# A two-layer encoder trunk in float32 on one core: SwiGLU's gate and up products by Strassen's seven products, and w_down applied in four parts over its rows

## The chip, the cores and the metric

One Trainium2 chip, and one of its cores. A core has TensorE (PE in the rows; its weight loads are the rows PEld), VectorE (DVE), ScalarE (ACT), GpSimd (POOL), and SyncE (SP), which here only issues transfers. SBUF is the working memory of the engines, PSUM the memory into which TensorE accumulates. The metric is the device time of one execution in microseconds.

## What is computed

Two layers on 512 tokens of width 1024, batch 1. Layer 0 mixes tokens with an mLSTM, layer 1 with dilated window attention. Behind each mixer comes the part that the change touches:

```python
def swiglu(xn, w_gate, w_up, w_down):
    return (jax.nn.silu(xn @ w_gate) * (xn @ w_up)) @ w_down
...
        h = h + mix
        h = h + swiglu(rms_norm(h, norm_ffn[i]), w_gate[i], w_up[i], w_down[i])
        gate = jax.nn.sigmoid(rms_norm(h, norm_ple[i]) @ ple_gate[i])
        h = h + gate * (p[i] @ ple_proj[i])
```

`w_gate` and `w_up` are 1024 x 2816, `w_down` is 2816 x 1024, all in float32, a pair for each layer.

## The kernel before

The residual lives transposed in eight tiles `hT` of 128 channels x 512 tokens. Every product is done in three passes (`mm3`): each float32 operand is split into a rounded part (`hi`, `wh`) and a remainder (`lo`, `wl`), and TensorE adds hi·hi, hi·lo and lo·hi. The weights are split on the way: SyncE loads a stretch of up to 1024 rows x 256 columns into one of three buffers `wst` (line 107), ScalarE writes `wh` (line 116), VectorE writes `wl = wst - wh` (line 117), and TensorE multiplies. `wh` and `wl` have three buffers each. A splitting can therefore run at most two products ahead of TensorE, and a load can start only when a `wst` buffer has been read for the last time.

`colproj` (line 510) is a projection over 256-column stretches of a weight; `Norm.add` (line 174) splits the new residual, scaled by the norm's weight, as soon as one of its tiles is done, and adds its squares up. The factor of the norm itself (one for each token) is applied behind the product: `stats` makes the sums by TensorE, `rsqrt_cols` (lines 236 to 240) finishes them on GpSimd, and `bcast` sends them through DRAM (tile `rbd`) and back as `rB`, one row repeated on all partitions.

`ffn` (line 539) goes over 11 pairs of 128-column blocks of gate and up (below: a cell, 256 columns of each). Each block is 8 k-steps x 3 passes = 24 matmuls of 512 columns; the gate block is scaled (L550) and put through Silu (L551), the up block scaled (L557), multiplied (L558) and split (L560, L561). All 22 resulting tiles stay in SBUF, and then `w_down` is one `colproj` over all of them (22 k-steps in one accumulation), whose result is added to `hT`. A scheduler puts the instructions of each engine in a fixed order; each engine then works its own list strictly in that order, and waits on semaphores.

Of the kernel before, what the change touches and what calls it, by code (L numbers as in the profile page):

```python
# [11 lines left out]
F32 = mybir.dt.float32  # L12
# [14 lines left out]
KT = D // P  # L27
# [5 lines left out]
WST = 3  # L33


@with_exitstack
def encoder_kernel(
# [40 lines left out]
    def ut(shape=(P, S), dt=F32, tag="u", bufs=62):  # L78
        return up.tile(list(shape), dt, tag=tag, name=nm(tag), bufs=bufs)
# [7 lines left out]
    def f(t):  # L87
        return t.bitcast(F32)
# [73 lines left out]
    class Norm:  # L162


        def __init__(self, wcol, btiles=False):
            self.wcol = wcol
            self.xh, self.xl = [], []

            self.btiles = btiles
            self.bh, self.bl = [], []  # L170
            self.q = None
            self.rcol = None

        def add(self, k, square=True):
# [7 lines left out]
            if self.btiles:  # L182
# [348 lines left out]
    nf = Norm(NW_FFN)  # L531
# [3 lines left out]
    nf.stats()  # L535
    nf.bcast()


    def ffn(l, n, nxt, rows=True):
        ah, al = [], []  # L540
        for j2 in range(JT // 2):
            sg = wload(w_gate[l], 0, KT, 256 * j2)
            su = wload(w_up[l], 0, KT, 256 * j2)
            for cc in range(2):
                og_ = ps()
                wh, wl = wcols(sg, KT, cc)
# [369 lines left out]
    nf = Norm(NW_FFN + 8)  # L916
# [3 lines left out]
    nf.stats()  # L920
    nf.bcast()
# [127 lines left out]
```

## Time and profile before

| | us |
|---|---|
| median of 3 runs | 1663.88 (1663.49 to 1666.16) |
| the profiled execution | 1660.66 |
| its span, from the first to the last instruction | 1659.0 |
| TensorE busy | 1616.1 (97%) |
| VectorE, ScalarE, GpSimd busy | 812.6, 602.6, 373.7 |

The span is what the rows below are counted in; the profiled execution's own time has 1.66 us more. Busy is the sum of the instructions' times; matmuls overlap in it, so that the distance between the starts of two matmuls, and not their duration, says how fast TensorE goes.

### The profile page before, as it was taken

Reading aid. Unit: us, or ns where it says so; the run is one execution under the profiler, and the core shown is the slowest. Engines: PE = TensorE matmul, PEld = TensorE weight load, DVE = VectorE, ACT = ScalarE, POOL = GpSimd, SP = SyncE. Lnnn points to the kernel's source line nnn. Section 1 sums busy time; section 2 is a strip of 40 time slices with the busy share of each in tenths; the row PEclk is TensorE's granted clock in tenths of the full one; section 3 lists DMA queues with packets and bytes.
Section 4 is the critical chain, followed back from the end, with each engine's and each line's share of the span. In section 5 each row is a group of like instructions: output and inputs, shape, how many; then the busy total and the mean of one; then the engine's idle time right before and its main releaser. Section 6 shows DMA issues by size and latency. Waiting matters only on the chain.

```text
span 1659.0 us, 20883 instructions
## 1 busy us (share of the span) xinstructions
PE 1616.1 (97%) x8324; PEld 1378.0 (83%) x8324; DVE 812.6 (49%) x1369; ACT 602.6 (36%) x1026; POOL 373.7 (23%) x479
## 2 busy tenths in 40 slices
PE   6999999999999998999999999999999999999997
PEld 5898998788888887777898988988887888888886
DVE  7655654644443322834645645545434444433253
ACT  5666543423232322623242422424333332323242
POOL 4455402000000100205707537165020000001100
PEclk9999999999999999999999999999999999999999
DMA  5322222422223223313323223223223232232231
GB/s 169 115 77 77 77 79 76 132 82 98 89 90 127 96 76 64 114 58 111 93 52 103 76 65 114 53 82 97 78 76 124 87 100 83 97 126 96 83 103 51
DMA packets 182753, 151.13 MB, mean 91 GB/s; under 512 B 17448, under 2 KB 173152, under 8 KB 182656
## 3 DMA queue, kind: packets, MB, share of 16 engines
q1 hardware_dynamic: 181520, 149.61, 29.5%
q8 instruction: 65, 1.06, 0.3%
q14 instruction: 32, 0.26, 0.1%
q10 hardware_dynamic: 1104, 0.13, 0.1%
q0 software_dynamic: 32, 0.07, 0.0%
HBM read 147.60 MB, written 2.19 MB: 90 GB/s over the span
## 4 chain that ended last, share of the span: by engine, by line
PE 86%; DVE 5%; DMA 5%; ACT 2%; POOL 1%; issue 1%; POOLq 0%; SPq 0%; DVEq 0%; ACTq 0%
PE pj L125 21%; PE pj L126 21%; PE pj L124 21%; PE o L124 5%; PE o L125 5%; PE o L126 5%; PE o L458 2%; PE o L890 2%; DMA rbd<-rs 1%; DVE wl L117 1%; DMA u<-rbd 1%; PE s L879 1%; DMA swo<-swd 1%; DMA u<-in_positions_dram 1%; PE s L124 0%
## 5 line engine op out<-in xcount | busy, mean ns | idle before, releaser
L126 PE MATMUL pj<-u,wl 128*128 128x512 f32 x1336 | 521.6, 390 | 5.3 <-DVE wl L117 5.3
L125 PE MATMUL pj<-u,wh 128*128 128x512 f32 x1336 | 521.8, 391 | 2.5 <-DVE u L179 2.5
L124 PE MATMUL pj<-u,wh 128*128 128x512 f32 x1336 | 522.0, 391 | 0.0
L116 ACT CAST wh<-wst 128x1024 fp32r<-128x1024 f32 (+2 forms) x267 | 271.1, 1018 | 665.2 <-PE pj L125 429.8
L117 DVE TENSOR_TENSOR wl<-wst,wh 128x1024 fp32r<-128x1024 f32 (+2 forms) x263 | 320.3, 1220 | 201.0 <-ACT wh L116 200.6
L126 PEld LDWEIGHTS pj<-u,wl 128*128 128x128 f32 x1336 | 251.1, 188 | 58.7 <-DVE wl L117 7.3
L125 PEld LDWEIGHTS pj<-u,wh 128*128 128x128 f32 x1336 | 251.1, 188 | 54.9 <-DVE u L179 3.3
L124 PEld LDWEIGHTS pj<-u,wh 128*128 128x128 f32 x1336 | 251.3, 188 | 51.5
L197 POOL TENSOR_TENSOR u<-u,u 128x512 f32<-128x512 f32 x30 | 51.6, 1721 | 862.1 <-ACT u L193 862.1
L124 PE MATMUL pj<-wh,u 128*128 128x256 f32 (+1 forms) x576 | 171.7, 299 | 5.3 <-DVE u L372 3.3
L125 PE MATMUL pj<-wl,u 128*128 128x256 f32 (+1 forms) x576 | 172.5, 299 | 2.7 <-DVE wl L117 2.7
L126 PE MATMUL pj<-wh,u 128*128 128x256 f32 (+1 forms) x576 | 172.2, 299 | 0.0
L124 PE MATMUL o<-u,wh 128*128 128x512 f32 x368 | 143.2, 389 | 0.0
L125 PE MATMUL o<-u,wh 128*128 128x512 f32 x368 | 143.2, 389 | 0.0
L126 PE MATMUL o<-u,wl 128*128 128x512 f32 x368 | 143.2, 389 | 0.0
L750 POOL TENSOR_TENSOR u<-u,RS 32x512 f32<-32x512 f32 x48 | 85.4, 1779 | 203.5 <-DVE u L749 202.9
L124 PEld LDWEIGHTS pj<-wh,u 128*128 128x128 f32 x576 | 111.7, 194 | 9.0 <-DVE u L372 3.5
L125 PEld LDWEIGHTS pj<-wl,u 128*128 128x128 f32 x576 | 111.9, 194 | 6.7 <-DVE wl L117 4.0
L126 PEld LDWEIGHTS pj<-wh,u 128*128 128x128 f32 x576 | 111.9, 194 | 2.5
L557 DVE TENSOR_TENSOR u<-o,u 128x512 f32<-128x512 f32 x44 | 30.4, 691 | 129.5 <-PE o L126 129.5
L124 PEld LDWEIGHTS o<-u,wh 128*128 128x128 f32 x368 | 69.1, 188 | 14.5
L125 PEld LDWEIGHTS o<-u,wh 128*128 128x128 f32 x368 | 69.2, 188 | 14.2
(278 smaller groups left out, 1718.8 us busy)
## 6 DMA issues: line engine op xcount, KB each, us to landing
wst<-in_b_w_in_dram SPq DMA_DIRECT2D x48, 512.0 KB, 3.8
wst<-in_w_gate_dram SPq DMA_DIRECT2D x22, 1024.0 KB, 5.2
wst<-in_w_up_dram SPq DMA_DIRECT2D x22, 1024.0 KB, 5.4
wst<-in_w_down_dram SPq DMA_DIRECT2D x16, 1024.0 KB, 5.1
wst<-in_b_w_in_dram SPq DMA_DIRECT2D x12, 1024.0 KB, 5.1
wst<-in_a_w_in_dram SPq DMA_DIRECT2D x8, 1024.0 KB, 5.3
wst<-in_ple_gate_dram SPq DMA_DIRECT2D x8, 1024.0 KB, 5.1
wst<-in_w_down_dram SPq DMA_DIRECT2D x8, 768.0 KB, 4.4
```

Source lines behind the costliest of these rows:

```text
L116: A.copy(hi, src)
L117: eng.tensor_tensor(lo, src, f(hi), op=ALU.subtract)
L124: T.matmul(o, ah, bh, start=start, stop=False)
L125: T.matmul(o, ah, bl, start=False, stop=False)
L126: T.matmul(o, al, bh, start=False, stop=stop_)
L197: (G if k < KT - 1 else V).tensor_tensor(self.q, self.q, s, op=ALU.add)
L458: T.matmul(o[:, d, :], pt[d][s][:, j * P:(j + 1) * P], vt[s][:, hh, :], start=s == ks[0], stop=s == ks[-1])
L557: V.tensor_tensor(u, ou, n.rB, op=ALU.mult)
L750: G.tensor_tensor(sh, sh, RS, op=ALU.mult)
L879: T.transpose(tp[:, i * P:(i + 1) * P], src[i // 2][:, i % 2, sel * P:(sel + 1) * P], ident)
L890: T.matmul(a_tile(o[e], i) if bi < 2 else b_tile(o[e], i), vv[i][:, e * P:(e + 1) * P], pt[:, i * P:(i + 1) * P], start=bi == 0 and i == 0 ...
```

## The change

**Gate and up.** For each cell and each k-row half, w11 and w12 are the upper and lower 512 rows of the 256 gate columns, w21 and w22 those of the up columns. The tokens are cut into two halves of 256. The eight products (two weights, two k halves, two token halves) become seven (Winograd's form): w11 and w12 with the first token half, w22 and four sums of weights with sums of quadrants of the input. A product is now 2 column blocks x 4 k-steps x 3 passes = 24 matmuls of 256 columns, and 7 of them make a cell. The four weight sums `s_[0]`, `s_[1]`, `s_[3]`, `s_[2]` (here S0, S1, S3, S2) are made by GpSimd, 128 x 1024 elements each, in three buffers `sw`; each is then split like a weight. The input's sums are made and split in `Norm.sums` while the projection ahead of the FFN runs. Partial results go back and forth between PSUM and VectorE.

**w_down** is applied after 3, 6, 9 and 11 cells, to the 6, 6, 6 and 4 tiles made so far; each part is scaled by `rB`, and added to `hT` (by GpSimd in the first three parts, by VectorE in the last). So the factor of the norm is no longer applied in the up block.

**rB** is made by TensorE and not through DRAM, inside the first cell.

The diff, without the tail of `Norm.__init__`, the two call sites of layer 1 (the same as those of layer 0) and blank lines:

```diff
-    def ut(shape=(P, S), dt=F32, tag="u", bufs=62):
+    def ut(shape=(P, S), dt=F32, tag="u", bufs=56):
...
+            if self.quads:
+                self.sums(k, h, w)
             if square:
                 self.square(k)
+        def sums(self, k, h, w):
+            e = ut()
+            A.activation(e, h, AF.Copy, scale=w)
+            self.e.append(e)
+            lo, hi = slice(0, 256), slice(256, S)
+            if k < 4:
+                d = ut((P, 256))
+                self.d = getattr(self, "d", []) + [d]
+                V.tensor_tensor(d, e[:, hi], e[:, lo], op=ALU.subtract)
+                if k % 2 == 0:
+                    self.pair1 = ut(dt=F32R), ut(dt=F32R)
+                th, tl = (t[:, 256 * (k % 2):256 * (k % 2) + 256] for t in self.pair1)
+                A.copy(th, d)
+                V.tensor_tensor(tl, d, f(th), op=ALU.subtract)
+                self.th[k][0], self.tl[k][0] = th, tl
+                return
+            j = k - 4
+            d2, d3, d4 = (ut((P, 256)) for _ in range(3))
+            V.tensor_tensor(d2, e[:, hi], self.d[j], op=ALU.subtract)
+            V.tensor_tensor(d3, e[:, hi], self.e[j][:, hi], op=ALU.subtract)
+            V.tensor_tensor(d4, e[:, lo], d2, op=ALU.subtract)
+            for i, d in ((1, d2), (2, d3), (3, d4)):
...
+                A.copy(th, d)
+                V.tensor_tensor(tl, d, f(th), op=ALU.subtract)
+                self.th[j][i], self.tl[j][i] = th, tl
...
-    nf = Norm(NW_FFN)
+    nf = Norm(NW_FFN, quads=True)
     colproj(a_w_out[0], mh, ml, KT, residual(nf), D)
-    nf.stats()
-    nf.bcast()
...
     def ffn(l, n, nxt, rows=True):
-        ah, al = [], []
-        for j2 in range(JT // 2):
-            sg = wload(w_gate[l], 0, KT, 256 * j2)
-            su = wload(w_up[l], 0, KT, 256 * j2)
...
-        pt = ple_in(l)
-        colproj(w_down[l], ah, al, JT, residual(nxt), D)
+        def product(o, w4, xs, start):
+            wh, wl = wsplit(w4, (P, 4, 256))
+            for cc in range(2):
+                for k in range(4):
+                    xh, xl = xs(k)
+                    c = slice(cc * P, cc * P + P)
+                    for i, (a, b) in enumerate(((wh, xh), (wh, xl), (wl, xh))):
+                        T.matmul(o[:, cc], a[:, k, c], b, start=start and cc + k + i == 0,
+                                 stop=k == 3 and i == 2, skip_group_check=True)
...
+        def parts(u, hf, a):
+            for cc in range(2):
+                ah, al = a[cc]
+                A.copy(ah[:, half[hf]], u[:, cc])
+                V.tensor_tensor(al[:, half[hf]], u[:, cc], f(ah[:, half[hf]]), op=ALU.subtract)
+        def first(j):
+            c = {}
+            sg = wload(w_gate[l], 0, KT, 256 * j)
+            su = wload(w_up[l], 0, KT, 256 * j)
+            c["w"] = w11, w12, w21, w22 = sg[:, 0:4], sg[:, 4:8], su[:, 0:4], su[:, 4:8]
+            s_ = [wp.tile([P, 4, 256], F32, tag="sw", name=nm("sw"), bufs=NSW) for _ in range(4)]
+            c["s"] = s_
+            G.tensor_tensor(s_[0], w21, w22, op=ALU.add)
+            G.tensor_tensor(s_[1], s_[0], w11, op=ALU.subtract)
+            G.tensor_tensor(s_[3], w12, s_[1], op=ALU.subtract)
+            G.tensor_tensor(s_[2], w11, w21, op=ALU.subtract)
+            c["r1"] = ps("s", (P, 2, 256), 3)
+            product(c["r1"], w11, lambda k: blk(k, 0), True)
+            c["s1"] = wide()
+            A.copy(c["s1"], c["r1"])
+            r5 = ps("o", (P, 2, 256), 2)
+            product(r5, s_[0], tsum(0), True)
+            c["s15"] = wide()
+            V.tensor_tensor(c["s15"], c["s1"], r5, op=ALU.add)
+            return c
+        def middle(c):
+            w11, w12, w21, w22 = c["w"]
+            s_ = c["s"]
+            c["a"] = [(ut(dt=F32R), ut(dt=F32R)) for _ in range(2)]
+            product(c["r1"], w12, lambda k: blk(4 + k, 0), False)
+            c["r6"] = ps("pj", (P, 2, 256), 3)
+            product(c["r6"], s_[1], tsum(1), True)
+            if n.rB is None:
+                n.bcast(by_pe=True)
+            c["g"] = g = [wide(), wide()]
+            V.tensor_tensor(g[0], c["r1"], cols(0), op=ALU.mult)
+            A.activation(g[0], g[0], AF.Silu)
+            v = wide()
+            V.tensor_tensor(v, c["s15"], c["r6"], op=ALU.add)
+            r3 = ps("s", (P, 2, 256), 3)
+            product(r3, s_[3], lambda k: blk(4 + k, 1), True)
+            V.tensor_tensor(v, v, r3, op=ALU.add)
+            V.tensor_tensor(g[1], v, cols(1), op=ALU.mult)
+            A.activation(g[1], g[1], AF.Silu)
+            product(c["r6"], s_[2], tsum(2), False)
+            u = wide()
+            V.tensor_tensor(u, c["s15"], c["r6"], op=ALU.add)
+            V.tensor_tensor(u, u, g[1], op=ALU.mult)
+            parts(u, 1, c["a"])
+        def last(c):
+            product(c["r6"], c["w"][3], tsum(3), False)
+            u = wide()
+            V.tensor_tensor(u, c["s1"], c["r6"], op=ALU.add)
+            V.tensor_tensor(u, u, c["g"][0], op=ALU.mult)
+            parts(u, 0, c["a"])
+            return c["a"]
+        def down(j0, a, final):
+            for c2 in range(D // 256):
+                st = wload(w_down[l], 256 * j0, len(a), 256 * c2)
+                for cc in range(2):
+                    o = ps()
+                    wh, wl = wcols(st, len(a), cc)
+                    for k in range(len(a)):
+                        mm3(o, wh[:, k], wl[:, k], *a[k], k == 0, k == len(a) - 1)
+                    t, h = ut(), hT[2 * c2 + cc]
+                    V.tensor_tensor(t, o, n.rB, op=ALU.mult)
+                    (V if final else G).tensor_tensor(h, t, h, op=ALU.add)
+                    if final:
+                        nxt.add(2 * c2 + cc)
+        chunks = ((0, 3), (3, 6), (6, 9), (9, JT // 2))
+        cell = first(0)
+        n.stats()
+        for j0, j1 in chunks:
+            a = []
+            for j in range(j0, j1):
+                middle(cell)
+                done_ = cell
+                if j + 1 < JT // 2:
+                    cell = first(j + 1)
+                a += last(done_)
+            if j1 == JT // 2:
+                pt = ple_in(l)
+            down(j0, a, j1 == JT // 2)
```

TensorE's order in a steady cell is: w12, S1, S3, S2, then w11 and S0 of the next cell, then w22. In the rows below a name ends in a number of its own, and behind a row stands the engine or the transfer queue (DMAHW) whose semaphore it waits for. Lines are those of the changed kernel where nothing else is said.

First VectorE, in the middle of layer 0's gate and up. Of the kernel before, one gate and one up block (L117 is a split):

```order
L117 TENSOR_TENSOR wl_3698<-wst_3624,wh_3697 128x1024 [waits Activation_49]
L561 TENSOR_TENSOR u_3621<-u_3617,u_3620 128x512 [waits Activation_49]
L550 TENSOR_TENSOR u_3657<-pj_3628,u_2970 128x512 [waits PE_49]
L117 TENSOR_TENSOR wl_3730<-wst_3626,wh_3729 128x1024 [waits Activation_49]
L557 TENSOR_TENSOR u_3689<-o_3660,u_2970 128x512 [waits PE_49]
L558 TENSOR_TENSOR u_3689<-u_3689,u_3657 128x512 [waits DVE_49,Activation_49]
```

And of the change, from the split of S2 to the split of the next cell's w12 (L118 is the split; 4559 and 4561 are the next cell's gate and up weights, 4563 its S0):

```order
L118 TENSOR_TENSOR wl_4525<-sw_4322,wh_4524 128x1024 [waits Activation_49]
L652 TENSOR_TENSOR u_4490<-u_4388,pj_4457 128x512 [waits PE_49]
L118 TENSOR_TENSOR wl_4573<-wst_4559,wh_4572 128x1024 [waits DMAHW5_49,Activation_49]
L656 TENSOR_TENSOR u_4490<-u_4490,s_4492 128x512 [waits DVE_49,PE_49]
L657 TENSOR_TENSOR u_4487<-u_4490,u_3296 128x512 [waits DVE_49]
L118 TENSOR_TENSOR wl_4604<-sw_4563,wh_4603 128x1024 [waits Activation_49]
L662 TENSOR_TENSOR u_4552<-u_4388,pj_4457 128x512 [waits PE_49]
L663 TENSOR_TENSOR u_4552<-u_4552,u_4487 128x512 [waits DVE_49,Activation_49]
L118 TENSOR_TENSOR wl_4634<-wst_4318,wh_4633 128x1024 [waits DMAHW4_49,Activation_49]
L613 TENSOR_TENSOR u_4426<-u_4552,u_4425 128x256 [waits Activation_49]
L613 TENSOR_TENSOR u_4428<-u_4552,u_4427 128x256 [waits Activation_49]
L118 TENSOR_TENSOR wl_4673<-wst_4559,wh_4672 128x1024 [waits PE_49,Activation_49]
```

Before, two splits come with four other operations (L550, L557, L558, L561), and a cell has two such sets; now seven splits and thirteen other operations make a cell, and the split of w22 (4634) stands behind two operations that need S2's product.

Second GpSimd, where layer 0's FFN begins. Before, the last square is followed at once by the norm's factor (L236 to L240):

```order
L197 TENSOR_TENSOR u_2688<-u_2688,u_2915 128x512 [waits Activation_49,Pool_49]
L236 TENSOR_TENSOR rs_533_2961<-ms_532_2959,nhalf 128x4 [waits DVE_49]
L237 TENSOR_TENSOR rt_534_2962<-rs_533_2961 128x4 [waits Pool_49]
```

In the change, the second cell's S0 and S1 (L623, L624) and the issue of the positions' load stand between the last square (L241) and the factor (L280 to L284), and S0 waits for a load:

```order
L626 TENSOR_TENSOR sw_3148<-wst_3142,wst_3144 128x1024 [waits DVE_49]
L241 TENSOR_TENSOR u_2696<-u_2696,u_2995 128x512 [waits Activation_49,Pool_49]
L761 DMA u_3071<-in_positions_dram 32x512 [waits PE_49]
L623 TENSOR_TENSOR sw_3375<-wst_3373 128x1024 [waits DMAHW2_49,DVE_49]
L624 TENSOR_TENSOR sw_3376<-sw_3375,wst_3371 128x1024 [waits DMAHW1_49,DVE_49,Pool_49]
L280 TENSOR_TENSOR rs_596_3223<-ms_595_3221,nhalf 128x4 [waits DVE_49]
```

In layer 1 only S0 of the second cell stands ahead of the factor.

Third ScalarE at the end of the second part of three cells, where w_down begins (4911 is the first w_down load, L612 splits the last cell's results):

```order
L117 CAST wh_4876<-wst_4561 128x1024 [waits DMAHW6_49,PE_49,Activation_49]
L612 CAST u_4668<-u_4795 128x256 [waits DVE_49]
L612 CAST u_4670<-u_4795 128x256
L630 COPY u_4843<-s_4814 128x512 [waits PE_49]
L117 CAST wh_4914<-wst_4911 128x768 [waits DMAHW1_49,Activation_49]
L117 CAST wh_4940<-wst_4911 128x768 [waits PE_49,Activation_49]
L612 CAST u_4668<-u_4904 128x256 [waits DVE_49]
```

Since the next cell's gate and up already hold two of the three `wst` buffers, all four w_down loads of a part use one and the same buffer, which is the one whose last reader is the split of w22 (`wh_4876` and its `wl`). Before, the first w_down loads came while three buffers took turns.

## Rows read from the trace of the kernel before

**Rows 1.** The page: busy time and share by engine, then the chain that ended last.

```profile
PE 1616.1 (97%) x8324; PEld 1378.0 (83%) x8324; DVE 812.6 (49%) x1369; ACT 602.6 (36%) x1026; POOL 373.7 (23%) x479
...
PE 86%; DVE 5%; DMA 5%; ACT 2%; POOL 1%; issue 1%; POOLq 0%; SPq 0%; DVEq 0%; ACTq 0%
```

**Rows 2.** Stages: stretch, its length, busy time of each engine, clock, DMA.

```profile
300.00:475.00 175.00, 175.00 (x774) 144.91 (x773) 84.39 (x102) 54.04 (x68) 0.00 (x0) 1.00 0.30 97
```

**Rows 3.** Timeline of PE: start, duration; 512-column matmuls in `ffn`, 56 steps apart.

```profile
559.77 0.39 PE L126 MATMUL pj<-u,wl 128*128 128x512 f32 x1
...
572.47 0.39 PE L125 MATMUL pj<-u,wh 128*128 128x512 f32 x1
```

**Rows 4.** Timeline of PE in layer 0's gate projection: 256-column matmuls, 13 steps apart.

```profile
199.75 0.28 PE L125 MATMUL pj<-wl,u 128*128 128x256 f32 x1
...
201.31 0.28 PE L126 MATMUL pj<-wh,u 128*128 128x256 f32 x1
```

**Rows 5.** Timeline of DVE in `ffn`: back-to-back operations.

```profile
342.47 0.69 DVE L558 TENSOR_TENSOR u<-u,u 128x512 f32<-128x512 f32 x1
343.08 1.22 DVE L117 TENSOR_TENSOR wl<-wst,wh 128x1024 fp32r<-128x1024 f32 x1
344.22 0.69 DVE L561 TENSOR_TENSOR u<-u,u 128x512 fp32r<-128x512 f32 x1
```

**Rows 6.** Groups by line in 300:475: busy us, mean ns, idle before.

```profile
L116 ACT CAST wh<-wst 128x1024 fp32r<-128x1024 f32 x33 | 34.7, 1053 | 106.8 <-PE pj L125 46.6 <-PE o L125 33.3 <-issue 26.9
```

**Rows 7.** Timeline of POOL, 14 to 36 us: the only wide two-input operations.

```profile
16.00 5.99 POOL L117 TENSOR_TENSOR wl<-wst,wh 128x1024 fp32r<-128x1024 f32 x2 [0.73 <-ACT wh L116]
27.05 2.40 POOL L117 TENSOR_TENSOR wl<-wst,wh 128x1024 fp32r<-128x1024 f32 x1 [5.07 <-ACT wh L116]
31.95 3.20 POOL L117 TENSOR_TENSOR wl<-wst,wh 128x1024 fp32r<-128x1024 f32 x1 [2.50 <-ACT wh L116]
```

**Rows 8.** Timeline of DVE in the same stretch.

```profile
15.73 1.22 DVE L117 TENSOR_TENSOR wl<-gst,wh 128x1024 fp32r<-128x1024 f32 x1
16.86 2.90 DVE L179 SCALAR_TENSOR_TENSOR u<-hT,nw,u 128x512 fp32r<-128x512 f32 x1
```

**Rows 9.** Timeline of POOL in layer 1's attention.

```profile
918.38 1.28 POOL L750 TENSOR_TENSOR u<-u,RS 32x512 f32<-32x512 f32 x1
919.74 2.15 POOL L752 TENSOR_TENSOR u<-u,u 32x512 f32<-32x512 f32 x1
...
923.21 1.29 POOL L752 TENSOR_TENSOR u<-u,u 32x512 f32<-32x512 f32 x1
```

**Rows 10.** Timeline of DVE in the same stretch.

```profile
918.91 1.84 DVE L117 TENSOR_TENSOR wl<-wst,wh 128x1024 fp32r<-128x1024 f32 x1
923.10 0.69 DVE L747 TENSOR_TENSOR u<-pj,RC 128x512 f32<-128x512 f32 x1 [2.35 <-PE pj L126]
```

**Rows 11.** DMA issues: size, median us from issue to landing.

```profile
wst<-in_w_up_dram SPq DMA_DIRECT2D x22, 1024.0 KB, 5.4
...
wst<-in_w_down_dram SPq DMA_DIRECT2D x8, 768.0 KB, 4.4
```

**Rows 12.** Timeline of PE: the two waits of the FFNs' first cells.

```profile
298.28 0.50 PE L126 MATMUL pj<-u,wl 128*128 128x512 f32 x1 [2.32 <-DVE wl L117]
...
1252.98 0.50 PE L126 MATMUL pj<-u,wl 128*128 128x512 f32 x1 [1.54 <-DVE wl L117]
```

**Rows 13.** Timeline of POOL after layer 0's mixer: the norm's factor.

```profile
276.84 1.02 POOL L236 TENSOR_TENSOR rs<-ms,nhalf 128x4 f32<-128x4 f32 x1 [6.36 <-DVE ms L233]
...
278.79 0.20 POOL L240 TENSOR_TENSOR rs<-rs,rt 128x4 f32<-128x4 f32 x1
```

**Rows 14.** Stages of PE after layer 0's FFN (length, busy, clock), then a wait there.

```profile
655.00:660.00 5.00, 1.86 (x9) 0.96 0.81 198
660.00:665.00 5.00, 3.30 (x7) 0.50 0.03 9
...
661.70 0.80 PE L126 MATMUL s<-u,wl 128*128 128x512 f32 x1 [4.85 <-DVE wl L117]
```

More of the change, by code (lines that the diff above doesn't have):

```diff
@@ L33 @@
 WST = 3
+NSW = 3
 @with_exitstack
@@ L162, in encoder_kernel, with __init__ @@
     class Norm:
-        def __init__(self, wcol, btiles=False):
+        def __init__(self, wcol, btiles=False, quads=False):
             self.wcol = wcol
+            self.quads = quads
+            self.e, self.th, self.tl = [], [[None] * 4 for _ in range(4)], [[None] * 4 for _ in range(4)]
             self.xh, self.xl = [], []
@@ L171, in __init__ @@
             self.q = None
-            self.rcol = None
+            self.rcol = self.rB = None
         def add(self, k, square=True):
@@ L187, in add @@
                 self.bl.append(bl)
+            if self.quads:
+                self.sums(k, h, w)
             if square:
                 self.square(k)
+        def sums(self, k, h, w):
[20 more added lines that the diff above has]
+            for i, d in ((1, d2), (2, d3), (3, d4)):
+                if i == 1:
+                    self.p12 = ut(dt=F32R), ut(dt=F32R)
+                if i == 3:
+                    if j % 2 == 0:
+                        self.p3 = ut(dt=F32R), ut(dt=F32R)
+                    th, tl = (t[:, 256 * (j % 2):256 * (j % 2) + 256] for t in self.p3)
+                else:
+                    th, tl = (t[:, 256 * (i - 1):256 * i] for t in self.p12)
+                A.copy(th, d)
+                V.tensor_tensor(tl, d, f(th), op=ALU.subtract)
+                self.th[j][i], self.tl[j][i] = th, tl
         def square(self, k):
@@ new lines, in ffn, with blk @@
+        half = (slice(0, 256), slice(256, S))
+        def blk(k, hf):
+            return n.xh[k][:, half[hf]], n.xl[k][:, half[hf]]
+        def product(o, w4, xs, start):
+            wh, wl = wsplit(w4, (P, 4, 256))
+            for cc in range(2):
+                for k in range(4):
[4 more added lines that the diff above has]
+                                 stop=k == 3 and i == 2, skip_group_check=True)
@@ new lines, in tsum, with cols, wide @@
+        def tsum(i):
+            return lambda k: (n.th[k][i], n.tl[k][i])
+        def cols(hf):
+            return n.rB[:, half[hf]].unsqueeze(1).to_broadcast([P, 2, 256])
+        def wide():
+            return ut((P, 2, 256))
+        def parts(u, hf, a):
[23 more added lines that the diff above has]
+            return c
```

23 lines of the change are left out of this document (1 added, 22 removed).

## The prediction

> **What bounds the kernel now.** I read the page's busy shares and the chain that ended last first: TensorE is busy 97% of the span and holds 86% of the chain [rows 1]. What to see there is that the work of the other engines costs time only where it makes TensorE wait. Then the stage that changes: in 175 us of gate and up TensorE stands still for nothing, VectorE has 84 us of work, ScalarE 54, GpSimd none [rows 2]. So this stage takes exactly as long as TensorE needs between matmuls. The distance between starts gives that: 512 columns (572.47 - 559.77)/56 = 0.2268 us [rows 3], 256 columns (201.31 - 199.75)/13 = 0.1200 us [rows 4]. A matmul of half the columns costs 53% of a whole one, not 50%.
>
> **TensorE's term.** A cell had 4 blocks x 24 = 96 matmuls, 96 x 0.2268 = 21.77 us. Now 7 products x 24 = 168, 168 x 0.1200 = 20.16 us. Over 11 cells in 2 layers this is 22 x 1.61 = 35 us less, if TensorE still never waits. w_down keeps its 22 x 3 x 8 = 528 matmuls of 512 columns in each layer; that term is 0.
>
> **What the other engines get for it.** The durations I take are distances between back-to-back operations: VectorE's split of 1024 elements 344.22 - 343.08 = 1.14 us, an operation of 512 elements 343.08 - 342.47 = 0.61 us [rows 5]; one of 256 is in no such row, I take half of 0.61 and a little, 0.35. GpSimd's addition of 1024 elements has one row that looks alone, 2.40 us; the others are 3.0 (5.99 for two) and 3.20 [rows 7]. In a cell:
> - VectorE: 7 splits x 1.14 + 9 x 0.61 + 4 x 0.35 = 14.9 us.
> - GpSimd: 4 x 2.40 = 9.6 us.
> - ScalarE: 7 casts of 1.05 [rows 6] and seven smaller operations, about 10.5 us by estimate.
>
> Each fits below 20.16 by itself. The question is whether VectorE and GpSimd can work side by side, since before GpSimd was idle here. The trace says which operations cannot. A split that starts at 918.91, while GpSimd is at work until 919.66, lasts 1.84 us and ends at 920.75, 1.09 after GpSimd's end; and the GpSimd operation issued at 919.74 lasts 2.15, that is until 921.89, 1.14 after that split was through [rows 9, 10]. GpSimd's next one, beside a VectorE operation that reads PSUM and one SBUF tile, lasts 1.29 as when alone, and so does the VectorE operation (0.69) [rows 9, 10]. So VectorE operations with two SBUF inputs and GpSimd's operations take turns, whole instructions at a time. And GpSimd gets its turn between two VectorE operations that follow each other directly: one waiting since 16.00 goes in behind the split that ends at 16.9, and the next VectorE operation lasts 2.90 [rows 7, 8]. The Trainium skill says the same (SBUF — State Buffer, "SBUF: two separate sides"): a pair of ports is locked for a whole instruction by GpSimd, or by VectorE with two SBUF inputs, and "the other fully blocks"; the trace agrees. By that page, too, the two are to be added and not laid side by side.
>
> In a cell VectorE's share of these turns is the 7 splits, three operations of 512 (L657, L663, L671) and four of 256: 7.98 + 1.83 + 1.40 = 11.2 us. With GpSimd's 9.6 the turns take 20.8 us: already more than TensorE's 20.16, and 0.96 under the old 21.77. That is the floor of a cell, 22 x 0.97 = 21 us less than before. Reaching it needs somebody to hold the turn at every moment, and a loop of dependences forbids that. The next cell's up weights go into the buffer of this cell's gate weights, so their load waits for GpSimd's S2, and for the split of w12. Then come: the load 5.4 us [rows 11]; S0, S1, S3, S2 with 9.6, each of which needs an `sw` buffer that VectorE's splits of S1, S3, S2 and S0 free; between and behind them, in VectorE's fixed order, the splits of S2, w11, S0, w22 and w12 (5 x 1.14 = 5.7), L657 and L663 (1.22) and two of 256 (0.7), each after GpSimd's current instruction. Sum 5.4 + 9.6 + 5.7 + 1.2 + 0.7 = 22.6 us for a cell. During the load VectorE does the rest of its list, so nothing is counted twice. In that loop TensorE waits for the splits of S0 and w22. I take 22.6: **22 x (22.62 - 21.77) = +19 us**. Bounds: 20.16 (-35) if it all hides; 25.0 (+71) if GpSimd's sums take the 3.0 us of the other row.
>
> **The ends of the parts.** In three parts of each layer the first w_down load waits for the split of w22, whose turn comes last in the loop, so that it is ready only when TensorE begins w22. Then load 4.4 [rows 11], cast 0.79 and split 0.86 (three quarters of 1.05 and 1.14), 6.05 us in all, against 2.88 us of w22's matmuls: TensorE waits 3.2 us, 6 times: **+19 us** (0 if that split is two products ahead; 6 x 6 if GpSimd's next sums hold up the last cell's results too, which on ScalarE stand behind the casts that wait for this load). The last parts load into free buffers; I take 1 us each, +2. The 24 more evictions and additions in a layer lie behind w_down tiles of 18 x 0.2268 = 4.08 us, where VectorE needs about 1.5 and GpSimd one 512-wide addition; nothing.
>
> **The FFN's start.** TensorE's list has the broadcast of rB ahead of the first cell's w12, and the norm's factor stands on GpSimd behind S0 and S1 of the second cell. From the end of the projection: the first up buffer is released about 2.5 us on, load 5.4, two sums 4.8, factor 2.2 (276.84 to 278.99) [rows 13]: 14.9 us. TensorE has three products and the sums of squares, 9.6 us, to do meanwhile: 5.3 us of waiting in layer 0 in place of 2.32, and with one sum less 2.9 in layer 1 in place of 1.54 [rows 12]: **+4 us**. After such a wait the clock drops: behind 4.85 us of standing still it was granted at 0.50, the lower of its two levels, for some 4 us, which cost about 2 us [rows 14]: +2 for layer 0 (up to +14, were it to drop at every part's end as well).
>
> **The input's sums** add per k ≥ 4 six VectorE operations of 256 to a projection whose tile takes 24 x 0.2268 = 5.4 us; with a weight sum of GpSimd in the same time the turns come to about 7. Most of the delay is taken up by the two products that are split ahead: +1 each, bounds 0 and 8. In the **last part** a tile takes only 12 x 0.2268 = 2.72 us, while the split of 512, two operations of 512, the next norm's split and GpSimd's square take some 3.2 of turns: 8 x 0.45 = 3.6, of which the tail shows perhaps 2 each.
>
> **Sum.** +19 + 19 + 2 + 4 + 2 + 2 + 4 = +52. Against the profiled execution's 1660.66 this is 1713; the median of the runs stands 3.2 above that execution, so 1713 to 1716. I say 1714.
>
> **Rivals.**
> - *TensorE stays the bound* (faster). Turns and loop fall into place beside the products, a cell takes 20.2 to 20.8, and the ends cost half: 1661 - 35 to -21, + 10 to 20 = 1636 to 1660. For it: each engine's own sum fits. Against it: 20.8 of turns. It decides at a cell of 21.77 - 33/22 = 20.3 us with my ends (33 us), or 21.0 with half of them. Chance 0.2.
> - *Half hidden* (slower). Cells of 21.5, ends half as dear: 1661 - 6 + 17 = 1672, with 1661 to 1690 around it. Chance 0.18.
> - *GpSimd at 3.0 us* (much slower). Sums as slow as the other row, and the clock falling at the parts' ends: 1714 + 52 + 12 = 1778. For it: two of the three rows; against it: those rows contain waiting for a turn, which I count already. Chance 0.08.
> - The forecast, cells of 22 to 23.5, has the rest, 0.54.
>
> **The numbers.** This measurement tells 0.2% (3.3 us) from no change. Faster holds the first rival, 0.2; same is the seam between the first two, 0.04; slower the rest, 0.76. The forecast's own range is 1692 to 1738. The whole range drops the lower half of the first rival and most of the third: 1648 to 1752.
>
> **What would show it.** In the changed kernel's stages of gate and up TensorE should no longer be busy without a gap; its waits should name the splits (L118) of w22 and S0, about 2.4 us a cell; sums L623 to L626 should take 2.4 when alone and longer beside a split; splits should have a mean well over 1.22; the distance from one cell's w12 to the next about 22.6. At the parts' ends a wait of 3 or so for the split of the first w_down load, in the first cell one for GpSimd's factor. I am wrong if the cells come at 20.2 with splits beside sums and no waits, or if the waits at the parts' ends are missing.

## The result and the profile after

The changed kernel takes 1730.18 us (median of 4 runs, 1727.44 to 1731.59) against 1665.02 us before on the same chip: 1.0398 of before, 95% interval 1.0383 to 1.0413. By the ratio the change costs 0.0398 x 1660.66 = 66 us, where 52 were forecast. The profiled execution is 1731.59 us with a span of 1729.9, 70.9 more than the span of before; the profiled execution of before, 1660.66 us, was 4.4 us shorter than the median given here, which is part of that.

The page of the changed kernel, the lines of [rows 1]:

```profile
PE 1619.8 (94%) x9924; PEld 1447.1 (84%) x9924; DVE 1165.4 (67%) x1691; ACT 708.0 (41%) x1222; POOL 680.5 (39%) x615
...
PE 50%; DVE 16%; issue 7%; DMA 5%; ACT 3%; POOL 1%; POOLq 0%; DVEq 0%; ACTq 0%; SPq 0%
```

TensorE holds 50% of the chain where it held 86%, VectorE 16% where it held 5%. VectorE's busy time rose by 353 us; how much of that is work and how much is standing inside an instruction is what the experiments have to tell.

Where the 70.9 us lie is read by cutting both programs at the same three operations of VectorE: the first eviction of a mixer's output projection (once per layer) and the first of the PLE. Stages of the kernel before, then of the changed one (stretch, length, busy time of PE, PEld, DVE, ACT, POOL, clock, DMA share, GB/s):

```profile
233.91:660.62 426.71, 420.62 (x1866) 347.42 (x1864) 180.84 (x223) 129.33 (x162) 25.73 (x23) 1.00 0.30 93
660.62:1190.06 529.44, 519.18 (x2915) 452.51 (x2916) 283.60 (x546) 190.45 (x377) 219.55 (x219) 0.99 0.29 84
1190.06:1659.00 468.94, 458.95 (x2072) 380.38 (x2070) 202.32 (x267) 147.11 (x201) 28.77 (x26) 0.99 0.29 93
```

```profile
233.74:696.92 463.18, 423.33 (x2670) 381.63 (x2668) 360.76 (x387) 182.91 (x261) 179.44 (x91) 0.97 0.27 86
696.92:1235.66 538.74, 520.53 (x2911) 454.31 (x2912) 281.36 (x544) 189.26 (x376) 219.37 (x219) 0.98 0.28 82
1235.66:1729.90 494.24, 457.86 (x2872) 412.22 (x2870) 377.47 (x428) 199.96 (x299) 181.95 (x94) 0.97 0.28 88
```

The stretch with layer 0's FFN is 36.5 us longer, that with layer 1's FFN and the end 25.3, and the PLE and attention between them, whose code is the same, 9.3. In the stretch between them TensorE's busy time grew by 1.4 us only: the rest is standing still.

Now one cell in the middle of a part, the stage of [rows 2], from one product u x g1 (L663) to the next. First the stage, then POOL's and DVE's timelines (start, duration, what ended an idle time before):

```profile
1409.79:1432.26 22.47, 21.30 (x176) 20.90 (x175) 21.64 (x21) 10.22 (x14) 10.84 (x5) 1.00 0.30 95
```

```profile
1421.89 2.41 POOL L623 TENSOR_TENSOR sw<-wst 128x1024 f32<-128x1024 f32 x1 [10.32 <-DMA wst<-in_w_up_dram]
1424.38 3.27 POOL L624 TENSOR_TENSOR sw<-sw,wst 128x1024 f32<-128x1024 f32 x1
1427.73 2.74 POOL L625 TENSOR_TENSOR sw<-wst,sw 128x1024 f32<-128x1024 f32 x1
1431.63 2.40 POOL L626 TENSOR_TENSOR sw<-wst,wst 128x1024 f32<-128x1024 f32 x1 [1.16 <-DVE wl L118]
```

```profile
1409.79 2.34 DVE L663 TENSOR_TENSOR u<-u,u 128x512 f32<-128x512 f32 x1
1412.05 1.21 DVE L118 TENSOR_TENSOR wl<-wst,wh 128x1024 fp32r<-128x1024 f32 x1
...
1423.03 2.36 DVE L118 TENSOR_TENSOR wl<-wst,wh 128x1024 fp32r<-128x1024 f32 x1 [0.32 <-ACT wh L117]
1425.31 0.68 DVE L656 TENSOR_TENSOR u<-u,s 128x512 f32<-128x512 f32 x1
1426.02 2.18 DVE L657 TENSOR_TENSOR u<-u,u 128x512 f32<-128x512 f32 x1
1428.12 3.43 DVE L118 TENSOR_TENSOR wl<-sw,wh 128x1024 fp32r<-128x1024 f32 x1
1431.48 0.68 DVE L662 TENSOR_TENSOR u<-u,pj 128x512 f32<-128x512 f32 x1
```

A split alone takes 1.21, and 2.36 or 3.43 when one of GpSimd's sums stands beside it; L657 and L663, 0.69 alone, take 2.18 and 2.34; the operations that read PSUM (L656, L662) keep their 0.68. GpSimd's sums lengthen in the same way, from 2.40 to 3.27. VectorE, which was busy for half of this stage before, has work or stands inside an instruction for 21.64 of 22.47 us. The waits of TensorE in the whole kernel (in all, times, longest) name the splits, the casts of the parts' first w_down loads, the PLE's evictions (L733), and GpSimd's factor. Of the 6.3 us for the factor 4.35 stand in layer 0's FFN and 2.0 at the start of the kernel; in layer 1's FFN TensorE does not wait for it.

```profile
PE pj L597 <- DVE wl L118: 20.8, 20, 2.8
PE pj L125 <- ACT wh L117: 19.5, 8, 3.0
PE pj L125 <- DVE u L733: 12.3, 3, 7.3
PE o L597 <- DVE wl L118: 8.9, 9, 1.5
PE s L255 <- POOL rs L284: 6.3, 2, 4.4
```

### The profile page after: what moved, and what is told of

Read it like the earlier page. It is cut to its first block, busy times and chain, and to the rows that moved or that the text cites. A ratio compares the mean times of both kernels' runs of the same rounds, so it can differ in the third digit from the quotient of the medians.

```text
span 1729.9 us, 25037 instructions
## 1 busy us (share of the span) xinstructions
PE 1619.8 (94%) x9924; PEld 1447.1 (84%) x9924; DVE 1165.4 (67%) x1691; ACT 708.0 (41%) x1222; POOL 680.5 (39%) x615
## 3 DMA queue, kind: packets, MB, share of 16 engines
HBM read 147.08 MB, written 2.18 MB: 86 GB/s over the span
## 4 chain that ended last, share of the span: by engine, by line
PE 50%; DVE 16%; issue 7%; DMA 5%; ACT 3%; POOL 1%; POOLq 0%; DVEq 0%; ACTq 0%; SPq 0%
PE pj L125 12%; PE pj L126 12%; PE pj L127 11%; DVE wl L118 7%; PE pj L597 6%; PE s L597 4%; DVE u L657 2%; ACT wh L117 2%; PE o L1027 2%; DMA wst<-in_w_down_dram 2%; DMA rbd<-rs 1%; DVE u L184 1%; DMA swd<-st 1%; PE s L1016 1%; DMA swo<-swd 1%
## 5 line engine op out<-in xcount | busy, mean ns | idle before, releaser
L118 DVE TENSOR_TENSOR wl<-wst,wh 128x1024 fp32r<-128x1024 f32 (+3 forms) x257 | 344.2, 1346 | 122.5 <-ACT wh L117 122.0
L125 PE MATMUL pj<-u,wh 128*128 128x512 f32 x984 | 391.7, 400 | 25.2 <-ACT wh L117 15.9
L126 PE MATMUL pj<-u,wh 128*128 128x512 f32 x984 | 389.0, 395 | 2.5 <-DVE u L184 2.5
L117 ACT CAST wh<-wst 128x1024 fp32r<-128x1024 f32 (+3 forms) x261 | 248.0, 961 | 349.9 <-PE pj L126 145.1
L127 PE MATMUL pj<-u,wl 128*128 128x512 f32 x984 | 389.7, 396 | 0.8 <-DVE wl L118 0.8
L597 PE MATMUL pj<-u,wh 128*128 128x256 f32 x1056 | 197.3, 286 | 6.3 <-ACT wh L117 5.6
L597 PE MATMUL s<-u,wh 128*128 128x256 f32 x1056 | 196.0, 286 | 0.0
L597 PE MATMUL pj<-u,wl 128*128 128x256 f32 x528 | 153.1, 290 | 20.8 <-DVE wl L118 20.8
L597 PEld LDWEIGHTS s<-u,wh 128*128 128x128 f32 x1056 | 167.7, 195 | 0.7
L118 DVE TENSOR_TENSOR wl<-sw,wh 128x1024 fp32r<-128x1024 f32 x88 | 151.1, 1717 | 8.0 <-ACT wh L117 7.8
L597 PE MATMUL s<-u,wl 128*128 128x256 f32 x528 | 151.0, 286 | 0.3 <-DVE wl L118 0.3
L241 POOL TENSOR_TENSOR u<-u,u 128x512 f32<-128x512 f32 x30 | 42.2, 1408 | 257.9 <-ACT u L237 257.9
L117 ACT CAST wh<-sw 128x1024 fp32r<-128x1024 f32 x88 | 92.4, 1050 | 115.8 <-PE s L597 47.8
```

Source lines behind the costliest of these rows:

```text
L117: A.copy(hi, src)
L118: eng.tensor_tensor(lo, src, f(hi), op=ALU.subtract)
L125: T.matmul(o, ah, bh, start=start, stop=False)
L126: T.matmul(o, ah, bl, start=False, stop=False)
L127: T.matmul(o, al, bh, start=False, stop=stop_)
L241: (G if k < KT - 1 else V).tensor_tensor(self.q, self.q, s, op=ALU.add)
```

## The experiments

The distance of a cell is below always that from one u x g1 on VectorE to the next; over a part's end the same distance holds a cell and a part of w_down, whose matmuls alone are 20.16 + 144 x 0.2268 = 52.8 us. In the changed kernel it is 22.2 to 23.2 us for most cells within a part, and 57.4 to 60.6 over an end, 59.0 in the mean of six. The kernel before takes 1653.8 to 1665.0 us on the chips that were used, so kernels are compared by their ratio to it on the same chip, and stretches of two profiles only to within some 2 us.

**1. The sums left out.**

```diff
-            s_ = [wp.tile(...) for _ in range(4)]
-            c["s"] = s_
-            G.tensor_tensor(s_[0], w21, w22, op=ALU.add)
...
+            c["s"] = s_ = [w21, w22, w22, w21]
```

> Leaves out GpSimd's four weight sums of each cell: the products that used them take a quadrant as loaded (the output is then not the reference's). Turns theory: with GpSimd out of the stage, VectorE's splits take 1.14 us each, TensorE no longer waits for the splits of S0 and w22, and a cell falls from 22.7 to the 20.16 us of its matmuls, at most 20.4: 22 x 2.4 = 53 us less, and some 6 less at the FFNs' starts, so about 1671 (1665 to 1682). The waits at the parts' ends stay, 2.5 us each. Rival, the load loop alone (the up load waits for a buffer whatever GpSimd does): the cell stays above 22 and the time above 1715. Rival, the price of 256-column matmuls: the cell stays where it is.

Measured: 0.9916 of before (0.990 to 0.9933), 1642 us on a chip where before took 1655. Against the changed kernel's ratio that is 0.048, some 80 us, where 59 were expected. The stage of one cell:

```profile
1359.75:1379.91 20.16, 20.16 (x171) 20.16 (x170) 15.76 (x20) 10.50 (x15) 0.00 (x0) 1.00 0.34 105
```

TensorE never stands still and the cell is exactly its 168 x 0.1200 = 20.16: 256-column matmuls cost what was forecast, and the load has no hold on the cell. What I had not expected: the ends fell too, from 59.0 to 53.7, 0.9 over their matmuls. The w_down load waits for the split of w22, and without any sums this is done early: at the first end 5.8 us before TensorE comes to w_down, where it is 3.0 in the changed kernel. So the ends' price was that of the sums as well.

**2. The sums on VectorE.** Four lines, `G.tensor_tensor(s_[...` becomes `V.tensor_tensor(s_[...`.

> The four sums of each cell go to VectorE (1.14 us each in place of 2.40). Turns theory: no turns are left, VectorE has 14.9 + 4 x 1.14 = 19.5 us a cell against TensorE's 20.16; but a sum that waits for the up load now holds up the splits behind it, so 20.3 to 21.3 us a cell and 1680 to 1700. Rival, GpSimd's sums only come late (no exclusion): faster too, but the mean of the splits of loaded weights stays where it was, whereas by the turns it falls to 1.14. Rival, the load loop: above 1715.

Measured: 1.0169 (1.0154 to 1.0184), 0.023 under the changed kernel, and the 1683 us lie in the range. A cell in layer 1:

```profile
1392.09:1412.25 20.16, 20.16 (x170) 20.16 (x170) 19.58 (x26) 10.32 (x14) 0.00 (x0) 1.00 0.32 105
```

VectorE's 19.58 us for the same sums fit under 20.16, where 14.9 of VectorE and 9.6 of GpSimd did not. The splits of loaded weights (128x1024) last 1302 ns in the mean of the whole kernel where they lasted 1491, against the rival that GpSimd's sums only come late. But six ends at 56.6 to 58.9 us remain, with TensorE waiting for the cast of the first w_down load (13.2 us in 9 waits in all).

**3. Half of the sums on VectorE.** S3 and S2 to VectorE, S0 and S1 stay.

> Only S3 and S2 go to VectorE, S0 and S1 stay with GpSimd. Turns theory: turns 11.2 + 2 x 1.14 + 2 x 2.40 = 18.3 us a cell, VectorE 17.2, the loop 22.6 - 4.8 + 2.3 = 20.1: TensorE is the bound but for scraps, 20.2 to 20.7 us a cell, 1675 to 1688. Rival, the first sums come late because their load does: S0 and S1 are as late as before, the cell stays at 22.7 and the time above 1720.

Measured: 1.0428 (1.0412 to 1.0443), no faster than with all four on GpSimd: the sum of turns, 18.3, says nothing about this kernel. DVE's timeline of a cell and its stage:

```profile
1404.24 1.23 DVE L118 TENSOR_TENSOR wl<-sw,wh 128x1024 fp32r<-128x1024 f32 x1
1410.21 1.23 DVE L625 TENSOR_TENSOR sw<-wst,sw 128x1024 f32<-128x1024 f32 x1 [4.75 <-POOL sw L624]
```

```profile
1394.91:1419.73 24.82, 21.59 (x159) 21.41 (x159) 17.94 (x23) 10.11 (x14) 5.85 (x2) 0.86 0.27 86
```

VectorE takes its instructions in order, and S3 needs GpSimd's S1: it stands 4.75 us in front of S3, and everything behind S3 with it, until TensorE waits for L652 (42.7 us in 16 waits in all). The rival had the time right and in part its reason: S0 begins 7.4 us after the issue of its load, and 6.7 in the changed kernel, though the profile names VectorE's L649 and not the load as what it waited for last. The rival did not have the cells: they do not stay at 22.7, most come 23.6 to 25.5 us apart, while the ends fall to 56.4 in the mean, so that the like total is a coincidence. What holds the cell here is a wait for a result, not for a turn.

**4. A fifth operation on GpSimd.**

```diff
             G.tensor_tensor(s_[2], w11, w21, op=ALU.subtract)
+            G.tensor_tensor(s_[2], s_[2], ones.unsqueeze(2).to_broadcast([P, 4, 256]), op=ALU.mult)
```

> One more GpSimd operation of 1024 elements in each cell, behind S2 (S2 times one, written to its place; no loaded buffer is held longer by it). The loop of dependences as I drew it: it falls into the 6 to 11 us in which GpSimd waits for the up load, where VectorE does the rest of its list, and the floor of turns rises to 20.8 + 2.4 = 23.2: +0.5 x 22 = 11 us, 1735 to 1755. Turns alone, all of them on the path: +2.4 x 22 = 53, 1783. Lateness alone, no exclusion: 0, 1730, and VectorE's splits as long as before.

Measured: 1.0653 (1.0635 to 1.0671), 0.0255 or 42 us over the changed kernel. The cells within a part, 24.6 to 25.0, grew by 2.4, the whole of the operation. GpSimd's and VectorE's timelines:

```profile
1342.89 2.22 POOL L627 TENSOR_TENSOR sw<-sw,ones 128x1024 f32<-128x1024 f32 x1
1355.05 3.03 POOL L623 TENSOR_TENSOR sw<-wst 128x1024 f32<-128x1024 f32 x1 [9.94 <-DMA wst<-in_w_up_dram]
```

```profile
1343.29 2.91 DVE L118 TENSOR_TENSOR wl<-wst,wh 128x1024 fp32r<-128x1024 f32 x1
```

My expectation of 11 us failed by its place: the added operation does end 9.94 us before GpSimd's next sum, but the split of w22 stands behind it (2.91 for 1.21), and behind that the split of w12, which lets the next up load go. In the loop as the prediction wrote it the operation belongs to the sum, 22.6 + 2.4 = 25.0.

**5. Seven small operations on GpSimd, at the same place.**

```diff
+            d_ = small((P, 4), "dum", 2)
+            G.tensor_tensor(d_, s_[2][:, 0, 0:4], s_[2][:, 0, 0:4], op=ALU.mult)
+            for _ in range(6):
+                G.tensor_tensor(d_, d_, d_, op=ALU.mult)
```

> The changed kernel with seven chained GpSimd products of 128x4 elements behind S2 of each cell (results unused), at the place in GpSimd's list where the fifth operation of 1024 elements stood; by the factor's rows (some 0.36 us from one to the next) about 2.5 us of GpSimd's time, with almost no data. Exclusion (a GpSimd operation costs the cell because VectorE may not run its two-input operations beside it, for as long as it moves data): at most 0.3 us a cell, ratio to before 1.039 to 1.044. Rival, lateness (whatever GpSimd does makes its next sums late, and these hold up the cell): 2.4 us a cell as the fifth operation, 1.06 to 1.07.

Measured: 1.0404 (1.038 to 1.0428), no difference from the changed kernel. POOL and DVE:

```profile
1421.80 0.53 POOL L628 TENSOR_TENSOR dum<-sw 128x4 f32<-128x4 f32 x1
1422.41 3.43 POOL L630 TENSOR_TENSOR dum<-dum 128x4 f32<-128x4 f32 x6
```

```profile
1422.20 1.21 DVE L118 TENSOR_TENSOR wl<-wst,wh 128x1024 fp32r<-128x1024 f32 x1
1423.33 0.75 DVE L613 TENSOR_TENSOR u<-u,u 128x256 fp32r<-128x256 f32 x2
1424.01 1.22 DVE L118 TENSOR_TENSOR wl<-wst,wh 128x1024 fp32r<-128x1024 f32 x1
```

GpSimd is held for 4 us, longer than by the fifth operation, and the splits beside it take 1.21 and 1.22. So it is not GpSimd's time that costs the cell but the wide operands: VectorE is shut out beside them, as the prediction read it from [rows 9, 10].

**6. A fourth buffer for loaded weights.** `WST = 3` becomes 4, `bufs=56` becomes 53; the sums stay with GpSimd.

> A fourth buffer for loaded weights (and 53 in place of 56 u buffers), the sums stay with GpSimd. It takes the load out of the loop: the next up weights no longer wait for the split of w12, and the first w_down load of a part has a buffer. Loop theory: the cell falls from 22.5 to the floor of the turns, 20.8 to 21.3, and the six ends lose some 3 us each: 1.3 x 22 + 18 = 47 us under the changed kernel, 1.011 to 1.016 of before. Rival, turns alone (VectorE's list in order, 14.9 of its own plus GpSimd's 9.6 less 2 of overlap, whenever the load lands): the cell stays at 22.3 to 22.5 and only the ends gain, 1.027 to 1.031.

Measured: 1.0293 (1.0279 to 1.0307), in the rival's range. Here the theory of the prediction falls. The up load still waits for a split, but for that of w22 in place of that of w12: it is issued 3.5 us after u x g1 (at 1397.52) where it was 5.4 in the cell shown above, and S0 begins 8.95 us after u x g1 where it was 12.10. So the loop is some 3 us shorter, and the cells are not: within a part they come 23.0 to 23.1 us apart, all but the first and the last of an FFN. The ends do go, to 55.2 to 55.4, a cell and 32.3. Stage, DVE and POOL of a cell:

```profile
1394.02:1417.11 23.09, 20.83 (x172) 20.45 (x171) 22.91 (x21) 10.01 (x14) 10.07 (x5) 1.00 0.29 93
```

```profile
1403.42 5.17 DVE L613 TENSOR_TENSOR u<-u,u 128x256 fp32r<-128x256 f32 x2
...
1409.11 1.21 DVE L118 TENSOR_TENSOR wl<-sw,wh 128x1024 fp32r<-128x1024 f32 x1
...
1410.84 3.10 DVE L118 TENSOR_TENSOR wl<-wst,wh 128x1024 fp32r<-128x1024 f32 x1
```

```profile
1402.97 2.79 POOL L623 TENSOR_TENSOR sw<-wst 128x1024 f32<-128x1024 f32 x1 [7.16 <-DMA wst<-in_w_up_dram]
...
1410.46 2.40 POOL L625 TENSOR_TENSOR sw<-wst,sw 128x1024 f32<-128x1024 f32 x1 [2.16 <-DVE wl L118]
1416.48 2.40 POOL L626 TENSOR_TENSOR sw<-wst,wst 128x1024 f32<-128x1024 f32 x1 [3.62 <-DVE wl L118]
```

VectorE is occupied for 22.91 of 23.09 us. Two operations of 256 elements, 0.75 together, take 5.17, each behind one of GpSimd's sums; one split takes 3.10 and one u x g1 2.33. With 4.4 + 1.9 + 1.6 us of standing, VectorE's own 14.9 make 22.8. VectorE itself is the limit: it does its own work and stands in front of most of GpSimd's, and S3 and S2 now wait 2.16 and 3.62 us for its splits.

**7. Only the parts.** The kernel before, with gate and up as they were, and w_down in four parts, whose additions VectorE makes:

```diff
+        def down(k0, xh, xl, final):
...
+            for j0, j1 in chunks:
+                if j2 + 1 == j1:
+                    if j1 == JT // 2:
+                        pt = ple_in(l)
+                    down(2 * j0, ah[2 * j0:], al[2 * j0:], j1 == JT // 2)
-        pt = ple_in(l)
-        colproj(w_down[l], ah, al, JT, residual(nxt), D)
```

> The kernel before with w_down in four parts and nothing else of the change: gate and up keep their 512-column products. If the price of a part's end lies in the new loop of buffers and turns (my theory): there is no such loop here, a part's first load finds a free buffer, and only the last parts' tails stay: 1.000 to 1.005 of before. Rival, the parts themselves cost what the ends cost in the changed kernel, 3 us and a lower clock, six times, and the tails: 1.012 to 1.02.

Measured: 1.0054 (1.004 to 1.0068), just over the upper edge. In the stretch with the first FFN TensorE waits 2.5 us for a split, where it waited 2.32 before, 0.9 us at the sums of squares, and at no part's end. Cut as above, the three stretches are 3.2, 6.5 and 1.9 us longer: most of the price lies in the PLE and attention, which nothing was done to.

**8. The factor ahead of the second cell's sums.**

```diff
+        late["factor"] = G.tensor_tensor(r, r, t, op=ALU.mult)
...
+            with tc.issue_after(late["factor"].ins) if j == 1 else nullcontext():
-            G.tensor_tensor(s_[0], w21, w22, op=ALU.add)
+                G.tensor_tensor(s_[0], w21, w22, op=ALU.add)
```

> The changed kernel, with GpSimd's S0 of the second cell put behind the norm's factor in GpSimd's list; nothing else. Start term as I predicted it: the broadcast no longer waits for S0 and S1, so TensorE's wait for the factor falls from 4.35 and 1.9 us to under 1, the sums of the second cell come 2.2 us later and are waited for by 1 to 2: 1 to 4 us less in each FFN, ratio to before 1.035 to 1.039. Rival, the factor is late because VectorE's mean of squares is (behind splits that wait for GpSimd's sums): the wait stays at 2 to 4 us and the time at 1.039 to 1.041.

Measured: 1.0389 (1.0375 to 1.0403), not to be told from 1.0398. TensorE's wait for the factor in layer 0 did fall, from 4.35 to 0.26 us; the 1.9 us of the expectation stand at the start of the kernel, not in layer 1's FFN. VectorE in the changed kernel, then in this one, whose line numbers are one higher here:

```profile
286.50 2.15 DVE L764 TENSOR_SCALAR u<-u,fcol 32x512 f32<-32x512 f32 x1
288.68 2.80 DVE L775 TENSOR_SCALAR u<-u 32x512 f32<-32x512 f32 x2
...
297.96 0.67 DVE L258 COPY u<-s 128x512 f32<-128x512 f32 x1
```

```profile
285.48 0.47 DVE L765 TENSOR_SCALAR u<-u,fcol 32x512 f32<-32x512 f32 x1
...
289.20 2.86 DVE L780 SCALAR_TENSOR_TENSOR RS<-u,RS 32x512 f32<-32x512 f32 x1
291.99 2.90 DVE L780 SCALAR_TENSOR_TENSOR RC<-u,RC 32x512 f32<-32x512 f32 x1
...
297.62 0.67 DVE L258 COPY u<-s 128x512 f32<-128x512 f32 x1
```

The copy of rB that every cell needs comes at 297.96 and at 297.62. In VectorE's list the position tables of the attention (L764 to L784) stand ahead of it, and S0 and S1 now hold up other rows of these tables. TensorE now waits 2.71 us for ScalarE's last operation on the tables. Both sides of my expectation were wrong about what is late: in layer 0 it is this list.

**9. Four buffers and the sums on VectorE.** Experiments 2 and 6 together.

> Four load buffers and all four sums on VectorE. Cells stay at the 20.2 us that they had with the sums on VectorE and three buffers; the six ends, 58.1 us from cell to cell there against 52.8 us of matmuls, fall to 53.5 to 54.5, since the first w_down load no longer waits for the split of w22: 6 x 4 = 24 us under the sums on VectorE alone, 1.0169 - 0.0145 = 1.002 of before (0.997 to 1.007). Rival, the ends wait for VectorE's line and not for the load: 58 stays, 1.017.

Measured: 0.9977 (0.9967 to 0.9987): a little faster than before. The ends are 53.1 to 53.4. The cells within a part, 19.5 to 21.2, are mostly a little longer than with three buffers (19.6 to 20.4 for most).

**10. The last part with three cells.**

```diff
-        chunks = ((0, 3), (3, 6), (6, 9), (9, JT // 2))
+        chunks = ((0, 2), (2, 5), (5, 8), (8, JT // 2))
```

> Four load buffers, sums on VectorE, and the parts cut as 2, 3, 3 and 3 cells in place of 3, 3, 3 and 2, so that a tile of the last part has 18 matmuls (4.08 us) over the next norm's work in place of 12 (2.72). The tail as I predicted it: the last part's waits of 0.3 to 0.7 us a tile go, 2 us in each FFN, and the first part, which has no norm behind it, hides its additions under 2.72 us: 0.9977 - 0.0024 = 0.995 of before. Rival: the additions of the first part on GpSimd now collide with VectorE's splits, and nothing is gained: 0.998.

Measured: 0.9933 (0.992 to 0.9946), the fastest version that leaves nothing out, 1643.49 us where before took 1655.1. The waits of 0.3 to 0.7 us at the last part's tiles are gone, as expected; and at the PLE's start TensorE waits 2.85 us where it waited 6.72 in experiment 9, which I had not counted.

## Why the prediction was right, and where it was not

Slower was forecast, and the change is slower, inside the range of 1648 to 1752 and of the forecast's own 1692 to 1738. The sum was 66 - 52 = 14 us too low. Experiment 1 cuts it in two. Without the sums the two FFN stretches (layer 0's to the PLE, layer 1's to the end) take 419.78 and 454.66 us, 21 less than before: what the prediction has of that kind is -35 for TensorE, +2 for the input's sums, +2 for the last parts and +4 for the tails, -27. With the sums the ratio rises from 0.9916 to 1.0398, 80 us of 1660.66: the prediction has 22 x (22.62 - 20.16) = 54 for the cells, 19 for the ends, 4 for the starts and 2 for the clock, 79. So the price of the sums was right as a whole, and that is in part luck: the cells and ends came out 8 us lower than forecast and the starts 11 us higher, as told below. Missing altogether was what the PLE and the attention between the FFNs lost, 9.3 us by the stages above.

- **TensorE's term** held: 0.1200 us a matmul, 20.16 a cell when nothing holds it up (experiments 1 and 2).
- **Turns** held, instruction by instruction: 2.40 alone and up to 3.27 beside a split, 1.21 and up to 3.43. Experiment 5 shows that it is the data and not GpSimd's time. The Trainium skill's sentence on the locked pair of ports, which the prediction weighed ("SBUF — State Buffer", "SBUF: two separate sides"), agrees with these rows of wide operations. The same sentence has a GpSimd operation lock the pair for as long as it lasts; in experiment 5 the splits keep 1.21 and 1.22 us beside its small operations, and there the measurement decides.
- **The loop of dependences** is the step that failed, though its 22.6 is what the cells came to (22.47 in the cell above). The prediction said that during the load VectorE does the rest of its list, so nothing counts twice, and that the loop with its load of 5.4 us sets the cell. With the loop some 3 us shorter the cell is 23.1 (experiment 6). VectorE's list in order is as long by itself: 14.9 of its own, and nearly 8 of standing in front of GpSimd's 9.6, because only six of its operations read PSUM and can run beside a sum. In the changed kernel both limits lie within a microsecond of each other; VectorE stands idle for 0.8 us of its cell there, and which of the two ends last in it is not settled. With a fifth sum it is the loop, 24.9, VectorE being idle for 2.2 us. The loop's own sum met 22.6 by two errors that cancel: the up load takes 6.4 us in the median and not 5.4, and the split of S2, which the loop counts with 1.14, falls into that load:

```profile
wst<-in_w_up_dram SPq DMA_DIRECT2D x22, 1024.0 KB, 6.4
...
1420.47 1.22 DVE L118 TENSOR_TENSOR wl<-sw,wh 128x1024 fp32r<-128x1024 f32 x1
```

- **The floor of 20.8** counted only the operations that take turns. VectorE can't jump over an operation that waits, so its PSUM operations count too unless a sum happens to fall beside them. That is why, of the ten cells within a part that are neither the first nor the last of an FFN, nine take 22.2 to 23.2 us and one 21.3, and why the rival that TensorE stays the bound fell.
- **The ends** were right in mechanism and size: TensorE waits 2.44 to 2.96 us at each, for the cast of a load that waits for w22's split, 3.2 forecast. The whole price is 59.0 - 22.5 - 32.7 = 3.8 us, 23 in all where the sum had 19. In the stages of five of the six ends the granted clock was 0.50 to 0.74, which the prediction had only in its upper bound; in the sixth, with a wait of 2.66 us, it stayed at 1.00, and why is not shown. Stages of three ends (the number behind GpSimd's is the granted clock):

```profile
362.00:368.00 6.00, 5.05 (x12) 3.69 (x13) 3.88 (x6) 2.28 (x4) 0.00 (x0) 0.52 0.31 104
466.00:472.00 6.00, 4.42 (x12) 3.25 (x13) 3.88 (x6) 2.28 (x4) 0.00 (x0) 0.72 0.28 73
...
1567.00:1573.00 6.00, 4.73 (x18) 3.24 (x19) 3.88 (x6) 2.28 (x4) 0.00 (x0) 1.00 0.30 101
```

- **The starts** are the term that was mis-sized. From the projection's first eviction (233.74, 1235.66) to the first u x g1 (309.63, 1307.30) the changed kernel takes 75.9 and 71.6 us, without the sums 65.1 and 60.0: 22 in all, for which the prediction has 11 (6 for the waits and the clock, and 2.5 for each first cell). In layer 0 it read the factor behind S0 and S1 rightly (4.35 us, 5.3 forecast) and took it for the cause; experiment 8 shows that VectorE's list would have been as late. In layer 1 it had 2.9 us of waiting for the factor, and there is none. What it had in neither layer is a wait for the cast and the split of the first cell's S1, 3.8 us in layer 0 and 4.9 in layer 1, which without the sums is missing; the clock behind it is granted at 0.50 (282 to 287 and 1285 to 1290 us). ScalarE has the casts of the input's sums ahead of S1's, and these wait for VectorE's L219, which takes 2.62 us beside GpSimd's S2 and 0.41 otherwise. TensorE in layer 1, and VectorE's L219 in layer 0:

```profile
1282.65 0.50 PE L597 MATMUL pj<-u,wh 128*128 128x256 f32 x2 [3.20 <-ACT wh L117]
1284.85 0.58 PE L597 MATMUL pj<-u,wl 128*128 128x256 f32 x1 [1.69 <-DVE wl L118]
...
273.23 2.62 DVE L219 TENSOR_TENSOR u<-u,u 128x256 f32<-128x256 f32 x1
```

- **Cells and ends together** came out lower than forecast: from the first u x g1 to the last 331.4 and 328.2 us, where 10 x 22.62 + 3 x (32.66 + 3.2) is 333.8.
- **The stages that were not touched** are in no term of the prediction. They are longer than the 529.44 us of before in the other kernels too, by 5.9 without the sums, 6.5 with the parts alone, 8.8 in experiment 9, 4.5 in experiment 10. In the changed kernel the waits of TensorE that lie in this stretch sum to 17.4 us in place of 8.9: 5.0 are for the PLE's L733, for whose like TensorE did not wait before, and in the attention it waits 5.6 us in place of 1.6 for splits of weights (L118). The longer wait at the PLE's start, 7.30 in place of 4.85, lies almost whole ahead of the cut. Within the attention VectorE's instructions stand in the same order as before, but for one copy. What shifts them was not tried and stays open.

## What to carry to other kernels

Before work is given to an idle GpSimd, count VectorE's list in order: its own time plus every wide GpSimd operation that it will stand in front of, not only the operations that take turns. Here four sums of 2.40 us on GpSimd made a cell of 22.5 us, while the same four on VectorE, 1.14 each, left it at 20.16, and moving half of them helped nothing, because an in-order engine then waited for the other half. An algorithm with an eighth fewer products is worth its additions only where an engine has room for them: the same Strassen step was 4.0% slower with the sums on GpSimd and 0.7% faster with them on VectorE, a fourth load buffer and a longer last part.

## What the runs showed of the hardware that was not expected

VectorE operations with a single SBUF tensor can be shut out as well: L764, a TENSOR_SCALAR from SBUF to SBUF on 32x512 elements, takes 0.47 us alone (L765 in experiment 8) and 2.15 beside S0, while operations with one SBUF and one PSUM input keep 0.68 beside the same sums. The Trainium skill ("SBUF — State Buffer", "SBUF: two separate sides") names a second case of the lock besides two SBUF inputs, VectorE's modes that use two ports; no run here shows in which mode L764 ran, but the rows agree with it.

Of small operations each takes its turn like a wide one: two of 256 elements that follow each other stood behind one sum each, 5.17 us for 0.75. What GpSimd's operations of 128x4 elements cost VectorE could not be measured: seven of them in a cell made no difference.
